# Odd mixer of a two-layer decoder trunk: when a block's result is split into its parts

## The chip, the cores and the metric

The kernel runs on one core of a Trainium2 chip (trn2). The metric is the device time of one launch in microseconds. All of it is one program with five engines: TensorE (PE; its weight loads are listed as PEld), VectorE (DVE), ScalarE (ACT), GpSimd (POOL) and SyncE (SP, which issues transfers). Each engine works through its own queue in order; semaphores tie the queues together.

## The reference

Two layers act on 256 positions of width 1024. Layer 0 has an attention and retention mixer, layer 1 the odd mixer, which the change touches. Each mixer is followed by a retrieval mixer ("peer").

```python
def short_conv_mixer(xn, w_in, conv_w, w_out):       # the odd mixer, layer 1; CONV_WIDTH is 3
    d = xn.shape[-1]
    bg, cg, hx = jnp.split(xn @ w_in, 3, axis=-1)
    u = cg * hx
    y = lax.conv_general_dilated(u, conv_w[:, None, :], window_strides=(1,),
                                 padding=[(CONV_WIDTH - 1, 0)],
                                 dimension_numbers=('NWC', 'WIO', 'NWC'),
                                 feature_group_count=d)
    return (bg * y) @ w_out

for layer in range(2):
    xn = rmsnorm(h, norm_mix[layer])
    h = h + (short_conv_mixer if layer % 2 else attn_retention_mixer)(xn, ...)
    h = h + peer(rmsnorm(h, norm_ffn[layer]), ...)
return rmsnorm(h, final_norm)
```

## The kernel before

The order on every engine is the order in which the program writes its instructions; no scheduler moves them.

**Weights.** All large matrices come through one stream of 128x1024 float32 tiles (class `Stream`). `_load` issues a tile's transfer from SP into one of eight `raw` buffers as soon as an earlier tile has given its buffer back. `_split` makes two parts of a tile: ScalarE casts it to a `hi` tile (line 146), and a subtraction of raw and `hi` gives a bfloat16 `lo` tile (line 148). The subtraction is on VectorE or, for tiles with a flag, on GpSimd. `next` hands a tile to a product and first calls `ahead`, which splits further tiles, up to four beyond the one that is asked for in this mixer.

**The products.** `u_tile` multiplies one weight tile with the 256 positions: 16 matmuls with `hi` (line 258), then 8 with `lo` (line 264). The result goes to a PSUM tile `hid`, of which there are two in turn; a product that needs one waits until VectorE has read the product before last in that ring.

**The odd mixer.** `odd_mixer` walks over 8 blocks of 128 channels. Block k takes three products, from the tiles 3k, 3k+1 and 3k+2 of its 24 input tiles. Tiles and products are given the same numbers here, so block 1 has the products 3, 4 and 5, and block 2 the products 6, 7 and 8. From tile 2 on the even tiles have their subtraction on VectorE and the odd ones on GpSimd.

- From product 3k VectorE makes `cg` (line 904).
- From product 3k+1 and `cg` it makes `u` (line 906), and from `u` the convolution `y` (lines 911 to 913).
- From product 3k+2 and `y` it makes `z` in PSUM (lines 918 and 919).
- `split_act` takes `z` apart: ScalarE casts it (`c2o`, line 653), VectorE subtracts that from `z` (line 656), and GpSimd makes a bfloat16 copy (`cbo`, line 658).

Block 0 is special: its first two products are run together by `u_pair` behind the end of the mixer before, its third follows, and three calls of `st.parts` split tiles 4, 5 and 6 between its steps. The third product of block 1 goes to another PSUM tile (`acc1`) instead of `hid`.

After the 8 blocks `v_phase` multiplies the parts of `z` with the 8 output tiles (lines 290 to 292), block by block, and the peer mixer of layer 1 follows.

Of the kernel before, what the change touches and what calls it, by code (L numbers as in the profile page):

```python
# [20 lines left out]
S = 256  # L21
D = 1024
ND = D // P
# [168 lines left out]
def trunk_kernel(ctx, tc, x, small, cst, mcst, ew_in, ew_out, ow_in, ow_out, wq, keys, pu, pv, pun, gains, out):  # L192
# [43 lines left out]
    def hid_tile(name):  # L236
        return ps_hid.tile([P, 512], F32, tag="hid", name=name)

    def side_tile(name):
        return ps_side.tile([P, 512], F32, tag="side", name=name)  # L240

    def acc_tile(n, name):
        return ps_acc.tile([P, 512], F32, tag=f"acc{n}", name=name)
# [3 lines left out]
    def nm(s):  # L247
        uid[0] += 1
        return f"{s}{uid[0]}"

    def u_tile(A2, Ab, ps=None, ahead=True):

        hi, lo = st.next(ahead)
        if ps is None:
            ps = hid_tile(nm("hid"))

        def one(k, s_):
            pe.matmul(ps[:, :S], hi[:, k * P:(k + 1) * P], A2[:, k, s_, :], start=k == 0 and s_ == 0, stop=False)  # L258

        for k in range(ND):  # L260
            one(k, 0)
            one(k, 1)
        for k in range(ND):
            pe.matmul(ps[:, :S], lo[:, k * P:(k + 1) * P], Ab[:, k, :], start=False, stop=k == ND - 1)  # L264
        return ps

    def u_pair(A2, Ab, tail, pss=None):


        ws = [st.next(ahead=False) for _ in range(2)]  # L270
        pss = pss or [hid_tile(nm("hid")) for _ in range(2)]
        for k in range(ND):
            for s_ in range(2):
                for (hi, lo), ps in zip(ws, pss):
                    pe.matmul(ps[:, :S], hi[:, k * P:(k + 1) * P], A2[:, k, s_, :], start=k == 0 and s_ == 0,
                              stop=False)
            tail(k)
        for (hi, lo), ps in zip(ws, pss):
            for k in range(ND):
                pe.matmul(ps[:, :S], lo[:, k * P:(k + 1) * P], Ab[:, k, :], start=False, stop=k == ND - 1)  # L280
        return pss
# [13 lines left out]
    def v_phase(n, part, each, norm):  # L295


        accs = [acc_tile(i, nm("acc")) for i in range(4)]
        for i in range(n - 2):
            each(i)  # L300
            w = st.next()
            p = part(i)
            for a in range(4):
                run(v_mm(w, p, accs[a], a // 2, a % 2, i == 0, False))
        each(n - 2)
        each(n - 1)
        ws = [st.next(), st.next(ahead=False)]
        st.ahead(0)
        ps = [part(n - 2), part(n - 1)]
        for a in range(4):  # L310
            for j in range(2):
                run(v_mm(ws[j], ps[j], accs[a], a // 2, a % 2, False, j == 1))
                if a == 3 and j == 0:
                    norm.amid()
            v.tensor_tensor(h[:, a // 2, (a % 2) * 512:(a % 2 + 1) * 512], accs[a],
                            h[:, a // 2, (a % 2) * 512:(a % 2 + 1) * 512], OP.add)
            norm.done(a, accs[a])
# [333 lines left out]
    def split_act(c2, cb, k, src, t, alone=False):  # L651

        act.copy(c2[:, k, 0, t], src)
        if alone:
            act.copy(cb[:, k, t], src)
        v.tensor_tensor(c2[:, k, 1, t], src, c2[:, k, 0, t].bitcast(F32), OP.subtract)
        if not alone:
            gp.tensor_copy(cb[:, k, t], c2[:, k, 0, t].bitcast(F32))
# [7 lines left out]
    def load_keys(l):  # L666
        KO = new_ko()
        for c in (slice(0, 4 * NK), slice(4 * NK, NPAIR * NK)):
            gp.dma_start(KO[:, c], keys[l][:, c])
# [211 lines left out]
    def odd_mixer(before, norm):  # L881
        with tc.tile_pool(name=nm("mix"), bufs=1) as mp, tc.tile_pool(name=nm("mix2"), bufs=2) as mp2:
            c2 = mp.tile([P, ND, 2, S], F32R, tag="c2", name="c2o")
            cb = mp.tile([P, ND, S], BF16, tag="cb", name="cbo")
            st.deep(mp2, 4 * ND, (1, 2))
            rs = mp.tile([P, 2, S], F32, tag="rs", name="rs")
            us = []
            for k in range(ND):
                w = [G[:, k * 3 + j:k * 3 + j + 1] for j in range(3)]
                if k == 0:  # L890
                    ps, pt = u_pair(xv["x2"], Xb, before.tail, [acc_tile(i, nm("hid")) for i in range(2)])
                    third = u_tile(xv["x2"], Xb, side_tile(nm("hid")), ahead=False)
                    rb = before.spread()
                    act.copy(rs[:, 0], rb)
                    v.tensor_tensor(rs[:, 1], rb, rs[:, 0], OP.mult)
                    load_keys(1)
                    us = [acc_tile(2 + i, nm("u"))[:, :S + 2] for i in range(2)]
                    for u in us:
                        v.memset(u[:, 0:2], 0.0)
                else:  # L900
                    ps = u_tile(xv["x2"], Xb)
                u = us[k % 2]
                cg = mp2.tile([P, S], F32, tag="cg", name=nm("cg"))
                v.tensor_tensor(cg, ps[:, :S], rs[:, 1], OP.mult)  # L904
                ps = u_tile(xv["x2"], Xb) if k else pt
                v.tensor_tensor(u[:, 2:], ps[:, :S], cg, OP.mult)
                if k == 0:
                    st.parts()
                    st.parts()
                y = mp2.tile([P, S], F32, tag="y", name=nm("y"))  # L910
                v.tensor_scalar(y, u[:, 0:S], w[0], None, op0=OP.mult)
                v.scalar_tensor_tensor(y, u[:, 1:S + 1], w[1], y, op0=OP.mult, op1=OP.add)
                v.scalar_tensor_tensor(y, u[:, 2:S + 2], w[2], y, op0=OP.mult, op1=OP.add)
                if k == 0:
                    st.parts()
                ps = u_tile(xv["x2"], Xb, acc_tile(1, nm("hid")) if k == 1 else None) if k else third
                z = (side_tile(nm("z")) if k else acc_tile(0, nm("z")))[:, :S]
                v.tensor_tensor(z, ps[:, :S], y, OP.mult)
                v.tensor_tensor(z, z, rs[:, 0], OP.mult)
                split_act(c2, cb, k, z, slice(0, S))  # L920

            def each(i):
                if i == 2:
                    norm.warm()

            v_phase(ND, lambda c: (c2[:, c, 0, :], c2[:, c, 1, :], cb[:, c, :]), each, norm)
# [575 lines left out]
    with tc.manual_schedule():  # L1502
        norms = [Norm(0)]
        nc.sync.dma_start(G, small)
        nc.sync.dma_start(C[:, :P], cst[:, :P])
        for th in range(2):
            (nc.scalar if th else nc.sync).dma_start(h[:, th, :], x[th])
        nc.sync.dma_start(C[:, P:], cst[:, P:])
        v.memset(Z, 0.0)
        act.activation(norms[0].w[:, 0, 6:7], Z[:, 0:1], AF.Sqrt)  # L1510
        for _ in range(3):
            st._load()
        busy(24)
        norms[0].first(hid_tile(nm("junk")))
        a = Norm(1)
        even_mixer(norms[0], a)
        b = Folded(2)
        peer(0, a, b)
        a = Norm(3)
        odd_mixer(b, a)  # L1520
        peer(1, a, Final(XF.rearrange("p k t -> p (k t)")[:, :D]))
# [38 lines left out]
```

## Time and profile before

| | |
|---|---|
| time, median of 3 runs (lowest to highest) | 1500.23 us (1499.57 to 1501.29) |
| time of the profiled execution | 1499.09 us |
| its span, first to last instruction | 1497.3 us |
| mean granted TensorE clock | 0.994 |
| busy share of the span: PE, DVE, ACT, POOL | 96%, 84%, 51%, 48% |
| blocks 1 to 7 of the odd mixer | about 775 to 838 us in the span |

Durations are from the one profiled execution. An entry in square brackets behind a row is the idle time of that engine before the row and what ended it.

### The profile page before, as it was taken

The page shows a single profiled execution, that of the slowest core. Times are in us where ns is not written, and L with a number is a line of the kernel's source. Part 1 is how long each engine was busy: PE and PEld are TensorE (multiplying, and loading weights), DVE is VectorE, ACT ScalarE, POOL GpSimd, SP SyncE. Part 2 cuts the span into 40 slices and gives each one's busy share as a digit, 9 for nine tenths or more (in the row PEclk, how much of TensorE's full clock was granted, in tenths as well). Part 3 has the DMA queues.
Part 4 walks back from the last instruction along what each step waited for, and adds up shares of the span by engine and source line. Part 5 has one row for each costly group of instructions (what it writes and reads, how often), then busy time and mean ns, then how long its engine had stood idle before and what let it go on. Part 6 is the DMA issues. An engine that isn't in the chain of part 4 may idle for free.

```text
span 1497.3 us, 30077 instructions
## 1 busy us (share of the span) xinstructions
PE 1437.4 (96%) x11158; PEld 1335.9 (89%) x11172; DVE 1251.5 (84%) x2469; ACT 761.5 (51%) x1825; POOL 725.1 (48%) x514
## 2 busy tenths in 40 slices
PE   9999999999999999999989999999999999999896
PEld 5667999999999998888888799999999999988885
DVE  5637999879998888888867589996999968888888
ACT  6556512257885545444563363212888835444454
POOL 6754545546665343444235364454566633434342
PEclk9999999999999999999999999999999999999999
DMA  8545899999999999999946578999999999999995
GB/s 321 196 153 201 301 391 408 397 409 403 408 405 408 403 399 409 409 401 408 394 174 209 185 250 320 408 408 397 407 407 399 409 398 402 401 408 406 397 405 225
DMA packets 147570, 532.99 MB, mean 356 GB/s; under 512 B 16992, under 2 KB 17248, under 8 KB 147424
## 3 DMA queue, kind: packets, MB, share of 16 engines
q1 hardware_dynamic: 72144, 258.36, 45.3%
q0 software_dynamic: 56704, 205.07, 34.8%
q10 hardware_dynamic: 18576, 67.64, 11.4%
q8 instruction: 88, 1.44, 0.4%
q14 instruction: 58, 0.48, 0.1%
HBM read 528.34 MB, written 1.05 MB: 354 GB/s over the span
## 4 chain that ended last, share of the span: by engine, by line
PE 39%; DMA 18%; DVE 17%; issue 16%; POOL 8%; ACT 3%; SPq 0%; POOLq 0%; ACTq 0%; DVEq 0%
PE hid L1356 17%; DMA raw<-pv 7%; POOL rows L964 5%; DMA rows<-pun,ig 4%; PE hid L258 3%; DMA grow<-pun,ig 2%; DVE rows L974 2%; POOL grow L964 2%; PE vo L1486 2%; DMA rows<-pv,ig 2%; PE ea L290 2%; PE ea L291 2%; PE ea L292 1%; PE hid L264 1%; PE vo L1482 1%
## 5 line engine op out<-in xcount | busy, mean ns | idle before, releaser
L1356 PE MATMUL hid<-xf,raw 128*128 128x160 f32 x3392 | 486.5, 301 | 6.4 <-DMA raw<-pu 4.0
L1356 PEld LDWEIGHTS hid<-xf,raw 128*128 128x128 f32 x3392 | 467.0, 191 | 9.0 <-issue 5.6
L1367 ACT CAST vhi<-raw 128x1024 fp32r<-128x1024 f32 x190 | 198.6, 1046 | 265.3 <-DMA raw<-pv 208.5
L1374 DVE TENSOR_TENSOR vlo<-raw,vhi 128x1024 bf16<-128x1024 f32 x190 | 231.9, 1223 | 81.3 <-ACT vhi L1367 58.8
L1486 PE MATMUL vo<-ko,vhi 128*128 128x320 f32 x1520 | 270.6, 320 | 26.8 <-DVE ko L1448 26.5
L964 POOL DMA_INDIRECT rows<-pv,ig x128 | 184.2, 1439 | 217.2 <-DVE gacc L989 179.8
L1486 PEld LDWEIGHTS vo<-ko,vhi 128*128 128x128 f32 x1520 | 224.4, 188 | 35.9 <-DVE ko L1448 35.4
L964 POOL DMA_INDIRECT rows<-pun,ig x128 | 169.4, 1324 | 135.7 <-DVE rows L974 65.6
L148 POOL TENSOR_TENSOR lo<-raw,hi 128x1024 bf16<-128x1024 f32 x70 | 168.5, 2417 | 83.2 <-ACT hi L146 80.1
L974 DVE SCALAR_TENSOR_TENSOR rows<-rows,xg 128x1024 f32<-128x1024 f32 x128 | 155.1, 1217 | 21.2 <-DMA rows<-pun,ig 17.9
L1389 ACT ACTIVATE hg<-hid 128x160 f32<-128x160 f32 (+14 forms) x240 | 62.5, 265 | 214.2 <-PE hid L1356 183.7
L989 DVE SCALAR_TENSOR_TENSOR gacc<-rows,ghid,gacc 128x1024 f32<-128x1024 f32 x124 | 158.6, 1279 | 1.1 <-DMA rows<-pv,ig 0.3
L1482 PE MATMUL vo<-hg,raw 128*128 128x160 f32 x1056 | 157.7, 302 | 0.8 <-DVE hg L1392 0.8
L964 POOL DMA_INDIRECT grow<-pv,ig x64 | 91.7, 1433 | 125.4 <-DVE gacc L989 115.6
L1482 PEld LDWEIGHTS vo<-hg,raw 128*128 128x128 f32 x1056 | 146.2, 191 | 1.2 <-DVE hg L1392 1.0
L1488 PE MATMUL vo<-hb,vlo 128*128 128x160 bf16 x1520 | 138.1, 234 | 0.0
L964 POOL DMA_INDIRECT grow<-pun,ig x64 | 81.2, 1268 | 78.1 <-DVE grow L974 45.0
L1488 PEld LDWEIGHTS <-vlo 128*128 128x128 bf16 x1520 | 100.5, 98 | 19.6 <-DVE vlo L1374 0.5
L1306 ACT ACTIVATE ko<-ko,idxT 128x128 f16<-128x128 f16 x320 | 101.7, 391 | 30.4 <-DVE ko L1292 30.3
L146 ACT CAST hi<-raw 128x1024 fp32r<-128x1024 f32 x100 | 102.3, 1047 | 17.4 <-issue 10.1
L258 PE MATMUL hid<-x,hi 128*128 128x256 f32 x800 | 107.4, 287 | 3.5 <-DVE cg L904 2.5
L258 PEld LDWEIGHTS hid<-x,hi 128*128 128x128 f32 x800 | 98.5, 190 | 4.5 <-ACT hi L146 2.7
(247 smaller groups left out, 2091.2 us busy)
## 6 DMA issues: line engine op xcount, KB each, us to landing
raw<-pu SPq DMA_DIRECT2D x212, 512.0 KB
raw<-pv SPq DMA_DIRECT2D x128, 512.0 KB
raw<-pv ACTq DMA_DIRECT2D x128, 512.0 KB
raw<-wq SPq DMA_DIRECT2D x32, 512.0 KB
raw<-ew_in SPq DMA_DIRECT2D x28, 512.0 KB
raw<-ow_in SPq DMA_DIRECT2D x24, 512.0 KB
hg<-pu SPq DMA_DIRECT2D x22, 512.0 KB
raw<-ew_out SPq DMA_DIRECT2D x8, 512.0 KB
```

The costliest lines, as they stand in the source:

```text
L146: self.nc.scalar.copy(hi, t)
L148: eng.tensor_tensor(lo, t, hi.bitcast(F32), OP.subtract)
L258: pe.matmul(ps[:, :S], hi[:, k * P:(k + 1) * P], A2[:, k, s_, :], start=k == 0 and s_ == 0, stop=False)
L964: gp.indirect_dma_start(self.row(s_), None, table, bass.IndirectOffsetOnAxis(IG[:, 0, s_ % STEPS:s_ % STEPS + 1].bitcast(U32), 0))
L974: v.scalar_tensor_tensor(r, r, 1.0, XG[:, q % 2, :], op0=OP.mult, op1=OP.mult, accum_out=w)
L989: v.scalar_tensor_tensor(self.acc[q], r, w, self.acc[q], op0=OP.mult, op1=OP.add)
L1356: pe.matmul(ps[:, :TD], w[k], XF[:, k, :], start=k == 0, stop=k == ND - 1)
L1367: act.copy(whi[j], raw)
L1374: v.tensor_tensor(wlo[j], raw, whi[j].bitcast(F32), OP.subtract)
L1482: pe.matmul(vo[b][:, :TD], w[:, b * P:(b + 1) * P], HG[:, i, :], stop=False, **m)
L1486: pe.matmul(vo[b][:, :2 * TD], hi[:, b * P:(b + 1) * P], hs, stop=i == NK - 1, **m)
L1488: pe.matmul(vo[b][:, :TD], lo[:, b * P:(b + 1) * P], hb, stop=i == NK - 1, **m)
```

## The change

The call of `split_act` for block k moves from the end of block k to block k+1, between that block's `cg` and its second product. The call for the last block stays behind the loop. No instruction is added or removed.

```diff
                 cg = mp2.tile([P, S], F32, tag="cg", name=nm("cg"))
                 v.tensor_tensor(cg, ps[:, :S], rs[:, 1], OP.mult)
+                if k:
+                    split_act(c2, cb, k - 1, z, slice(0, S))
                 ps = u_tile(xv["x2"], Xb) if k else pt
                 v.tensor_tensor(u[:, 2:], ps[:, :S], cg, OP.mult)
...
                 v.tensor_tensor(z, ps[:, :S], y, OP.mult)
                 v.tensor_tensor(z, z, rs[:, 0], OP.mult)
-                split_act(c2, cb, k, z, slice(0, S))
+            split_act(c2, cb, ND - 1, z, slice(0, S))
```

## Prediction

> **What bounds the kernel now.** I read the page first, then the windows around the odd mixer, then who waits for whom there, then each engine's timeline, row by row.
>
> ```profile
> span 1497.3 us, 30077 instructions
> ```
> ```profile
> 775.00:793.00 18.00, 14.47 (x120) 13.14 (x119) 14.70 (x25) 9.50 (x12) 11.68 (x9) 1.00 0.75 264
> 793.00:838.00 45.00, 45.00 (x386) 42.81 (x385) 31.22 (x52) 16.58 (x20) 22.98 (x14) 1.00 0.61 199
> 860.00:880.00 20.00, 19.74 (x161) 18.14 (x161) 16.62 (x65) 15.24 (x33) 12.92 (x10) 1.00 0.50 172
> 960.00:1000.00 40.00, 40.00 (x290) 40.00 (x290) 39.73 (x148) 8.35 (x21) 21.50 (x17) 0.98 1.03 409
> 1000.00:1100.00 100.00, 100.00 (x791) 99.50 (x791) 84.22 (x190) 54.28 (x192) 52.37 (x44) 1.00 1.03 403
> ```
>
> The columns are the stretch, its length, the busy time of PE, PEld, DVE, ACT and POOL, the granted clock, the DMA share and GB/s. From 793 to 838 us PE is busy for 45.00 of 45.00 us: nothing that moves on another engine can shorten that, and ScalarE's waits there cost nothing. Only from 775 to 793 us, in blocks 1 and 2, does PE stand still. So the waits view of 775 to 842 us has to be read with that in mind:
>
> ```profile
> ACT c2o L653 <- DVE z L919: 30.4, 8, 4.6
> PE hid L258 <- DVE cg L904: 2.5, 1, 2.5
> PE hid L258 <- DVE u L906: 1.0, 1, 1.0
> ```
>
> ScalarE's 30.4 us look like the prize, but PE's own waits are two, and they set the scale. PE's timeline (start, duration; each row is the `hi` half of a product) gives products 5, 6, 7, 8, 9 and, last, 12:
>
> ```profile
> 780.17 2.15 PE L258 MATMUL hid<-x,hi 128*128 128x256 f32 x16
> ...
> 783.24 2.15 PE L258 MATMUL hid<-x,hi 128*128 128x256 f32 x16
> ...
> 787.30 2.15 PE L258 MATMUL hid<-x,hi 128*128 128x256 f32 x16 [1.03 <-DVE u L906]
> ...
> 792.81 2.15 PE L258 MATMUL hid<-x,hi 128*128 128x256 f32 x16 [2.47 <-DVE cg L904]
> ```
> ```profile
> 795.60 2.15 PE L258 MATMUL hid<-x,hi 128*128 128x256 f32 x16
> ...
> 803.98 2.15 PE L258 MATMUL hid<-x,hi 128*128 128x256 f32 x16
> ```
>
> Undisturbed, a product starts 795.60 - 792.81 = 2.79 us behind the one before. Measured by that, product 6 is late by 0.28 us, product 7 by 1.27 and product 8 by 2.72: 4.27 us in all, the most that this change can win in the mixer. Product 7 takes the PSUM buffer that `u` of block 1 reads, product 8 the one that `cg` of block 2 reads. So the end is set by how early VectorE reaches these two.
>
> **What holds VectorE there.** Its rows are, in order: subtraction for tile 6, last step of z(0), cg(1), subtraction for tile 8, u(1), last step of z(1), subtraction for tile 10, cg(2).
>
> ```profile
> 779.09 2.00 DVE L148 TENSOR_TENSOR lo<-raw,hi 128x1024 bf16<-128x1024 f32 x1
> ...
> 781.46 0.43 DVE L919 TENSOR_TENSOR z<-z,rs 128x256 f32<-128x256 f32 x1
> ...
> 782.68 0.41 DVE L904 TENSOR_TENSOR cg<-hid,rs 128x256 f32<-128x256 f32 x1
> 784.23 2.58 DVE L148 TENSOR_TENSOR lo<-raw,hi 128x1024 bf16<-128x1024 f32 x1 [1.14 <-ACT hi L146]
> 786.73 0.42 DVE L906 TENSOR_TENSOR u<-hid,cg 128x256 f32<-128x256 f32 x1
> ...
> 789.29 0.43 DVE L919 TENSOR_TENSOR z<-z,rs 128x256 f32<-128x256 f32 x1
> ...
> 791.10 1.23 DVE L148 TENSOR_TENSOR lo<-raw,hi 128x1024 bf16<-128x1024 f32 x1 [0.52 <-ACT hi L146]
> 792.25 0.42 DVE L904 TENSOR_TENSOR cg<-hid,rs 128x256 f32<-128x256 f32 x1
> ```
>
> On ScalarE: casts of tiles 4, 5, 6; c2o(0); casts of 7, 8, 9; c2o(1); casts of 10, 11, 12.
>
> ```profile
> 775.13 2.95 ACT L146 CAST hi<-raw 128x1024 fp32r<-128x1024 f32 x3
> 781.93 0.37 ACT L653 CAST c2o<-z 128x256 fp32r<-128x256 f32 x1 [3.85 <-DVE z L919]
> 782.20 2.94 ACT L146 CAST hi<-raw 128x1024 fp32r<-128x1024 f32 x3
> 789.75 0.37 ACT L653 CAST c2o<-z 128x256 fp32r<-128x256 f32 x1 [4.61 <-DVE z L919]
> 790.02 2.94 ACT L146 CAST hi<-raw 128x1024 fp32r<-128x1024 f32 x3
> ```
>
> On GpSimd: subtraction for tile 5; cbo(0); subtractions for 7 and 9.
>
> ```profile
> 777.21 2.80 POOL L148 TENSOR_TENSOR lo<-raw,hi 128x1024 bf16<-128x1024 f32 x1 [0.77 <-ACT hi L146]
> 782.36 0.40 POOL L658 CAST cbo<-c2o 128x256 bf16<-128x256 f32 x1 [2.36 <-ACT c2o L653]
> 783.33 5.74 POOL L148 TENSOR_TENSOR lo<-raw,hi 128x1024 bf16<-128x1024 f32 x2 [0.56 <-ACT hi L146]
> ```
> ```profile
> 798.21 2.40 POOL L148 TENSOR_TENSOR lo<-raw,hi 128x1024 bf16<-128x1024 f32 x1 [0.56 <-ACT hi L146]
> ```
>
> The last row, tile 13, shows one such subtraction by itself, 2.40 us.
>
> So the casts of tiles 7 to 9 sit behind c2o(0), which waits for z(0); VectorE's subtraction for tile 8 waits for the second of them; it then takes 2.58 us where the one for tile 10 takes 1.23; and the subtraction for tile 10 again waits for a cast behind c2o(1). The 2.58 us are an exclusion: 1.22 us of VectorE's work between two subtractions of GpSimd gives 5.74 - 1.22 = 4.52 us for the two, 2.26 each, and 783.33 + 2.26 + 1.22 = 786.81 = 784.23 + 2.58. The two engines do not do these subtractions at once, and VectorE, waiting, got its turn before GpSimd's next one. Tile 6 shows the same: GpSimd ends at 780.01, VectorE 1.08 us later. [...]
>
> **The change part by part.** The same instructions are issued, and SP's and PE's orders stay as they are. ScalarE: per block one cast, of tile 3k+4, goes ahead of c2o(k-1), so the order becomes 4, 5, 6, 7; c2o(0); 8, 9, 10; c2o(1); 11. VectorE: `cg` of block k goes ahead of the subtraction for `c2o` of block k-1, and where tile 3k+4 is even, its `lo` does too. GpSimd: where tile 3k+4 is odd, its `lo` goes ahead of cbo(k-1). The transfers that wait for freed raw buffers only come earlier.
>
> *Cast of tile 7.* ScalarE is free at 775.13 + 2.95 = 778.08. The tile must be there:
>
> ```profile
> 758.65 1.28 SPq L131 DMA_DIRECT2D raw<-ow_in  x3
> 769.12 0.33 SPq L131 DMA_DIRECT2D raw<-ow_in  x1
> ```
> ```profile
> GB/s 342 80 15 0 259 360 375 284 120 7 0 0 0 178 288 0 0 0 11 269 353 308 422 406 306 397 317 29 226 324 284 240 251 73 320 160 248 255 273 149
> ```
>
> The second row has 40 slices of 1.125 us from 755 us on. Slices 5 to 9 carry 1398 x 1.125 = 1573 KB, the three tiles 7, 8 and 9, in by 765.1; slices 14 and 15 carry tile 10, in by 771.9. The cast runs from 778.08 to about 779.1.
>
> *Tile 7 on GpSimd.* It is ready at 779.1, but GpSimd is busy until 780.01 and VectorE waits since 779.09. With VectorE served first, as for tile 8 today, tile 6 still ends at 781.09 and z(0) at 781.89; tile 7 follows, 781.09 + 2.36 = 783.45 (2.36 lies between the 2.26 and the 2.40 from above).
>
> *Block 1.* cg(1) follows z(0) at once, about 781.92, so product 6 starts at its undisturbed 782.96. c2o(0) stays at 781.93, the cast of tile 8 takes the place of tile 7's at 782.20 and ends at 783.2. VectorE's subtraction for tile 8 finds GpSimd done at 783.45 and takes about 1.1, as for tile 6: it ends at 784.57, and u(1) starts at about 784.5 instead of 786.73. That is 0.98 us from the cast and 1.3 from the exclusion. Product 7 starts undisturbed at 785.75, behind u(1)'s end at 784.9.
>
> *Block 2.* u(1) to the end of z(1) takes 789.72 - 786.73 = 2.99 us of dependent steps: z(1) ends at 787.5. Tile 10's cast now runs right behind 8 and 9 and ends at 785.2 (its buffer is tile 5's, which product 5 reads until 782.32). So the subtraction for tile 10 starts at 787.5 instead of 791.10, if GpSimd's for tile 9 (from 784.57 + 0.40 for cbo(0), to about 787.4) is over. cg(2) starts 1.15 later, at 788.65 instead of 792.25: 3.6 us earlier, and product 8 with it, at 789.2.
>
> *What can shave it.* [...] No row shows who wins between a short cast and a waiting VectorE. The bounds are 2.9 and 3.6; I take half of the 0.40 off the upper: 3.4. This leaves PE 0.87 us of its 4.27.
>
> *What is moved and hidden.* The subtraction for c2o(k-1) now stands ahead of `u`, 0.42 us, and it waits for c2o, which stands behind a cast that waits for a `hi` buffer. That buffer is freed by product 3k-1, which z(k-1) needs as well, so the cast is over first. The cover in the later blocks:
>
> ```profile
> 799.12 2.58 DVE L148 TENSOR_TENSOR lo<-raw,hi 128x1024 bf16<-128x1024 f32 x1
> 801.62 0.42 DVE L906 TENSOR_TENSOR u<-hid,cg 128x256 f32<-128x256 f32 x1
> ```
>
> Here, in block 3, a collision of tile 14 with tile 13 on GpSimd already costs 1.36 us (2.58 - 1.22) and u(3) ends at 802.04, 1.94 us before product 12 needs its buffer at 803.98. So 0.42 us, or one collision in a block, is free; two in one block would stop PE by 2 x 1.36 - 1.94 = 0.78. c2o of the last block keeps its place, and `v_phase` needs the parts of block 6 long after.
>
> **Sum.** From product 9 on everything depends on PE's queue, the output products and the peer mixer included, so it moves as a whole. The profiled execution of 1499.09 us (span 1497.3, 1.8 around it) becomes 1495.7; that run lies 1.1 under the median of 1500.23, so the median becomes 1496.8. A difference of 0.2%, 3.0 us, is about what a measurement of this kernel can tell from no change; the forecast lies just beyond it.
>
> **The rivals.** [...] Chance 0.13.
>
> *The gain is lost in the transfers.* From 960 us the DMA share is 1.03 at 409 GB/s, and a stage bound by transfers ends when they do. For it: that stage is most of the rest. Against it: at 860 to 880 us the share is 0.50, so the bound stage does not begin by itself, but when buffers come free,
>
> ```profile
> SPq L131 <- POOL lo L148: 43.1, 15, 5.9
> ```
>
> and these come earlier with the rest (the row is SP's waits from 755 to 860 us). If it holds all the same, 1500.2. Chance 0.12.
>
> *Slower: second collisions.* [...] Chance 0.05.
>
> **How the numbers follow.** The forecast has 0.70. Its own range is 2.9 to 3.6 us, widened by the runs' spread (0.66 below the median, 1.06 above). The low end is the full 4.27 of PE's stalls, 1496.0, less 0.3 of spread: 1495.7. The high end takes in the first rival: 1499.2; the other two, 0.17, are left out. Faster by over 3.0 us: about three quarters of 0.70 and a little of luck elsewhere, 0.54. Within 0.2%: the rest of it, the first two rivals and half of the third, 0.42. Slower by over 0.2%: 0.04.
>
> **What would show it.** In the changed profile product 6 follows 5 by 2.79 us, 7 follows 6 by 2.79, and 8 follows 7 by 3.2 to 4.2; VectorE's subtraction for tile 8 takes about 1.2 us; a cast stands between 778 and 779.1 us; PE is full from product 9 to the end of the mixer. [...] The prediction is wrong if the gaps go and the time stays, or if new gaps stand behind product 9.

## The result, and the profile after

The changed kernel took 1495.57 us (median of 11 runs, 1494.1 to 1497.11) against 1499.89 us for the kernel before in the same comparison (11 runs, 1497.86 to 1503.21): ratio 0.9972, 95% interval 0.9964 to 0.998, so 4.3 us less. Forecast were 1496.8 us and a range from 1495.7: the direction and the size were right, the time lies 0.13 us under the range's low end.

The windows of the mixer in the changed kernel (busy time of PE, PEld, DVE, ACT, POOL; granted clock; DMA share; GB/s):

```profile
775.00:793.00 18.00, 17.51 (x151) 16.53 (x151) 15.00 (x29) 10.62 (x15) 15.86 (x9) 1.00 0.77 278
793.00:838.00 45.00, 45.00 (x379) 42.12 (x377) 27.64 (x51) 18.57 (x22) 22.98 (x15) 1.00 0.58 199
```

PE is busy for 17.51 of the first 18 us, where it was 14.47. The waits from 775 to 842 us:

```profile
ACT c2o L653 <- DVE z L921: 13.3, 8, 3.8
...
PE hid L258 <- DVE cg L904: 0.5, 1, 0.5
DVE c2o L656 <- ACT c2o L653: 0.4, 1, 0.4
```

ScalarE's wait for z fell by 17 us, far more than the kernel won. VectorE's waits for c2o, 0.44 us in each block, all but went; in the kernel before their row was

```profile
DVE c2o L656 <- ACT c2o L653: 3.5, 8, 0.4
```

The 3.1 us by which they fell lie close to what the kernel won, so they are a rival for its cause; an experiment below takes them away alone. PE's own two waits are now one of 0.5 us. PE's timeline, products 5 to 8:

```profile
781.77 2.15 PE L258 MATMUL hid<-x,hi 128*128 128x256 f32 x16
...
784.56 2.15 PE L258 MATMUL hid<-x,hi 128*128 128x256 f32 x16
...
787.35 2.15 PE L258 MATMUL hid<-x,hi 128*128 128x256 f32 x16
...
790.88 2.14 PE L258 MATMUL hid<-x,hi 128*128 128x256 f32 x16 [0.49 <-DVE cg L904]
```

Products 6 and 7 follow after 2.79 us each, undisturbed; product 8 after 3.53, so 0.74 us late. The delays went from 4.27 to 0.74 us: 3.53 won. Product 5 itself starts 1.60 us later than in the profile before. All of that lies ahead of what the change touches: product 2 already starts at 772.94 instead of 771.34. So the spans differ by 2.0 us only, and a comparison of the two spans would have hidden nearly half of the gain.

VectorE (subtraction for tile 8, u(1), last step of z(1), subtraction for tile 10, cg(2)), then ScalarE, then GpSimd:

```profile
784.88 1.48 DVE L148 TENSOR_TENSOR lo<-raw,hi 128x1024 bf16<-128x1024 f32 x1 [0.52 <-ACT hi L146]
786.29 0.42 DVE L908 TENSOR_TENSOR u<-hid,cg 128x256 f32<-128x256 f32 x1
...
788.84 0.43 DVE L921 TENSOR_TENSOR z<-z,rs 128x256 f32<-128x256 f32 x1
789.18 1.22 DVE L148 TENSOR_TENSOR lo<-raw,hi 128x1024 bf16<-128x1024 f32 x1
790.31 0.42 DVE L904 TENSOR_TENSOR cg<-hid,rs 128x256 f32<-128x256 f32 x1
```
```profile
776.73 3.90 ACT L146 CAST hi<-raw 128x1024 fp32r<-128x1024 f32 x4
783.53 0.37 ACT L653 CAST c2o<-z 128x256 fp32r<-128x256 f32 x1 [2.91 <-DVE z L921]
783.80 2.95 ACT L146 CAST hi<-raw 128x1024 fp32r<-128x1024 f32 x3
```
```profile
778.81 6.13 POOL L148 TENSOR_TENSOR lo<-raw,hi 128x1024 bf16<-128x1024 f32 x2 [0.22 <-ACT hi L146]
784.89 0.39 POOL L658 CAST cbo<-c2o 128x256 bf16<-128x256 f32 x1
```

Four casts now stand in front of the first c2o instead of three. Tile 8's subtraction starts right behind its cast and takes 1.48 us instead of 2.58; tile 10's starts behind z(1) without waiting for anything. GpSimd's tiles 5 and 7 take 6.13 us, two subtractions with VectorE's tile 6 between them: without its 1.22 us they leave 2.45 us each, and tile 6 ends at 782.69, 2.25 us ahead of GpSimd's 784.94. So the waiting VectorE was served first, as for tile 8 in the kernel before.

### The profile page after: what moved, and what is told of

Same layout as the page of the kernel before. It is cut to its first block, busy times and chain, and to the rows that moved or that the text cites. A ratio compares the mean times of both kernels' runs of the same rounds, so it can differ in the third digit from the quotient of the medians.

```text
span 1495.3 us, 30076 instructions
## 1 busy us (share of the span) xinstructions
PE 1436.5 (96%) x11158; PEld 1334.2 (89%) x11172; DVE 1247.0 (83%) x2469; ACT 760.6 (51%) x1825; POOL 730.8 (49%) x514
## 4 chain that ended last, share of the span: by engine, by line
PE 38%; DMA 18%; DVE 17%; issue 16%; POOL 8%; ACT 2%; another core or an unknown queue 0%; SPq 0%; POOLq 0%; DVEq 0%; ACTq 0%
PE hid L1358 17%; DMA raw<-pv 8%; POOL rows L966 5%; PE hid L258 4%; DMA rows<-pun,ig 3%; DMA grow<-pun,ig 3%; DVE rows L976 3%; POOL grow L966 2%; DMA rows<-pv,ig 2%; PE vo L1488 2%; DMA raw<-pu 2%; PE ea L290 2%; PE hid L264 2%; PE ea L291 2%; PE ea L292 1%
## 5 line engine op out<-in xcount | busy, mean ns | idle before, releaser
L966 POOL DMA_INDIRECT rows<-pv,ig x128 | 188.6, 1474 | 214.6 <-DVE gacc L991 174.0
L1308 ACT ACTIVATE ko<-ko,idxT 128x128 f16<-128x128 f16 x320 | 101.8, 390 | 52.6 <-DVE ko L1294 52.4
L1311 ACT ACTIVATE ko<-ko,idxT 128x128 f16<-128x128 f16 x320 | 101.1, 387 | 0.0
```

The source lines that it names most:

```text
L966: gp.indirect_dma_start(self.row(s_), None, table, bass.IndirectOffsetOnAxis(IG[:, 0, s_ % STEPS:s_ % STEPS + 1].bitcast(U32), 0))
```

## The experiments

All are compared with the kernel before, on one chip per group. "Mixer" is the time from the start of product 5 to the first output product (line 290) in the run's profile, read from PE's timeline; "delays" are the times by which products 6, 7 and 8 follow later than 2.79 us. The ratio with its interval is the one on record; it is not exactly the quotient of the two medians.

| run | delays, us | mixer, us | median, us (kernel before) | ratio, 95% interval |
|---|---|---|---|---|
| kernel before | 0.28, 1.27, 2.72 | 57.33 | | |
| changed, first comparison | 0, 0, 0.74 | 53.79 | 1495.57 (1499.89) | 0.9972 (0.9964 to 0.998) |
| again | 0, 0, 0.73 | 53.80 | 1496.50 (1501.32) | 0.9970 (0.996 to 0.998) |
| again2 | 0, 0, 0.72 | 53.78 | 1497.37 (1500.92) | 0.9978 (0.9969 to 0.9988) |
| rest_only | 0, 1.54, 2.72 | 57.32 | 1500.59 (1501.32) | 0.9997 (0.9986 to 1.0008) |
| cast_only | 0.27, 0, 0.78 | 54.13 | 1496.56 (1501.32) | 0.9965 (0.9952 to 0.9978) |
| cg_first | 0, 0, 0 | 54.79 | 1496.44 (1501.32) | 0.9967 (0.9956 to 0.9979) |
| cg_first_b2 | 0, 0, 0 | 53.07 | 1496.58 (1500.76) | 0.9972 (0.9962 to 0.9983) |
| null | 0.27, 1.28, 2.72 | 57.32 | 1499.89 (1500.76) | 1.0001 (0.999 to 1.0012) |
| pad | 0, 0, 0.73 | 107.56 | 1550.88 (1500.76) | 1.0329 (1.0316 to 1.0343) |
| pad2 | 0, 0, 0.72 | 57.64 | 1500.93 (1500.92) | 1.0005 (0.9994 to 1.0015) |
| idle | 0, 0, 0.73 | 69.24 | 1516.60 (1500.92) | 1.0103 (1.0083 to 1.0122) |

**Which part does it.** The call was taken apart. `rest_only` leaves ScalarE's cast where it was and moves the two other instructions:

```diff
+                if k:
+                    split_act(c2, cb, k - 1, z, slice(0, S), cast=False)
                 ps = u_tile(xv["x2"], Xb) if k else pt
...
-                split_act(c2, cb, k, z, slice(0, S))
+                split_act(c2, cb, k, z, slice(0, S), rest=False)
+            split_act(c2, cb, ND - 1, z, slice(0, S), cast=False)
```

> One part alone: ScalarE's cast of z stays where it was, only VectorE's subtraction and GpSimd's copy move one product later. Theory A says the gain comes from ScalarE's next weight cast getting ahead of the cast of z: product 6 loses its 0.28 us of delay, but u of block 1 still waits for tile 8, whose cast still comes third behind c2o, so products 7 and 8 start as before: 0 to 0.3 us under the kernel before. The rival (VectorE's wait of 0.44 us for c2o in front of cg is what counts, 8 x 0.44 = 3.5 us in sum) says about 3.5 us.

`cast_only` leaves all three at the end of the block, but has the next weight tile split ahead of them:

```diff
+                if k < ND - 1:
+                    st.ahead(1)
                 split_act(c2, cb, k, z, slice(0, S))
```

> The other part alone: the parts of z stay at the end of their block, but the split of the next weight tile (its cast, and its subtraction) is written ahead of them. Theory A: tile 8's and tile 10's casts come one place earlier as in the changed kernel; cg of block 2 still stands behind VectorE's subtraction for c2o of block 1 (0.42 us), so product 8 is 0.3 to 0.5 us later than in the changed kernel: 3.0 us under the kernel before. The rival (VectorE's waits) says about 0.

The waits of `rest_only` from 775 to 843 us:

```profile
ACT c2o L654 <- DVE z L924: 30.5, 8, 4.6
...
DVE lo L148 <- ACT hi L146: 8.7, 6, 1.7
...
PE hid L258 <- DVE cg L907: 2.5, 1, 2.5
...
PE hid L258 <- DVE u L911: 1.3, 1, 1.3
...
DVE c2o L659 <- ACT c2o L654: 0.4, 1, 0.4
```

In the kernel before the second of these rows was

```profile
DVE lo L148 <- ACT hi L146: 5.1, 7, 1.7
```

VectorE's wait for c2o has all but gone (3.5 to 0.4 us, one wait in place of eight), its wait for the `hi` casts has grown (5.1 to 8.7 us), and PE still waits for `cg` and for `u`. `rest_only` won nothing: product 6 wins its 0.28 us, product 7 loses it again, the mixer stays at 57.32 us, the ratio is 0.9997. `cast_only` shortens the mixer by 3.20 us of the changed kernel's 3.54, and its time cannot be told from the changed kernel's; its product 8 comes only 0.04 us later than there, where 0.3 to 0.5 us were expected. `rest_only` and the changed kernel differ in ScalarE's order alone. So the gain comes from one ScalarE cast per block getting ahead of the cast of z, and moving the parts of z is one way to get that. VectorE's waits of 0.44 us for c2o, 3.5 us in sum and thus as long as the gain, are worth nothing: what they free, VectorE spends waiting for the cast behind.

**What is left.** `cg_first` also moves the split of tile 3k+4 behind `cg`; `cg_first_b2` does so in block 2 alone:

```diff
-                    ps = u_tile(xv["x2"], Xb)
+                    ps = u_tile(xv["x2"], Xb, ahead=False)
...
                 if k:
+                    st.ahead(0)
                     split_act(c2, cb, k - 1, z, slice(0, S))
```

> The changed kernel, with the split of tile 3k+4 written behind cg of block k instead of ahead of its product, still ahead of the parts of z. In the changed kernel product 8 is the only one that still waits (0.74 us), for cg of block 2, which stands behind the subtraction for tile 10. Theory A: cg of block 2 comes about 1.1 us earlier, product 8 starts undisturbed, and all of the 4.27 us are gone: 0.7 us under the changed kernel, 4.3 under the kernel before, with u of block 2 still ahead of product 9. If the subtraction of tile 10 is only late somewhere else, the delay shows up before product 9 or 10 and the time equals the changed kernel's.

> The changed kernel with the later split in block 2 alone, so that the collisions of the later blocks stay as they are in the changed kernel. Theory A: product 8 starts 2.79 us behind product 7 (3.53 in the changed kernel), no gap of PE comes after it, and the mixer is 0.74 us shorter than in the changed kernel, 4.27 us shorter than before; time 0.7 us under the changed kernel, which is about 0.05% and hard to see in the times. If the collision comes back whatever the block, there is a gap of 1 to 2 us before a product between 9 and 18.

Product 8 loses its last delay in both, but in `cg_first` product 16 then follows product 15 after 4.51 us, 1.72 too late. Its PE, VectorE and GpSimd rows show why:

```profile
812.91 2.15 PE L258 MATMUL hid<-x,hi 128*128 128x256 f32 x16 [1.47 <-DVE z L921]
```
```profile
803.44 3.40 DVE L148 TENSOR_TENSOR lo<-raw,hi 128x1024 bf16<-128x1024 f32 x1
...
808.99 3.43 DVE L148 TENSOR_TENSOR lo<-raw,hi 128x1024 bf16<-128x1024 f32 x1
```
```profile
803.38 2.38 POOL L148 TENSOR_TENSOR lo<-raw,hi 128x1024 bf16<-128x1024 f32 x1 [1.30 <-ACT hi L146]
808.96 2.38 POOL L148 TENSOR_TENSOR lo<-raw,hi 128x1024 bf16<-128x1024 f32 x1 [3.20 <-ACT hi L146]
```

Twice in one block GpSimd's subtraction starts 0.06 and 0.03 us ahead of VectorE's, which then ends 1.08 us behind the end of GpSimd's: 3.4 us instead of 1.22, 2.2 more each time, where the prediction had 1.36 us as the price of a collision. Two collisions in one block are what the prediction's paragraph on the cover priced at 0.78 us; here they cost 1.72. Two subtractions of GpSimd ahead of one of VectorE's do not show here. `cg_first_b2` has no such gap and the shortest mixer of all, 53.07 us. That is 4.26 us under the kernel before; by time, 0.9972, it cannot be told from the changed kernel.

**Does the mixer's time reach the end, and is there more?** The first comparison's 4.3 us against 3.5 us in the trace led to these three, and to the two repetitions of the changed kernel.

> The changed kernel once more, unaltered. Theory A (the mixer alone): PE's three delays before products 6, 7 and 8 shrink from 4.27 us to about 0.74 us, the rest of the program only moves, so the time is 3.5 us under the kernel before (about 0.24%), and the 4.3 us of the first comparison were scatter. Theory B (the later stages add to it): the time stays 4.3 us or more under it (0.29% or more).

> The kernel before against itself, unaltered. It shows how far apart two medians of one kernel lie in this measurement: ratio 1.000, and an interval of about 0.1% to either side if the two comparisons of the changed kernel (4.3 and 4.8 us) are 3.5 us and scatter. If it lies off 1.000 by 0.05% or more, the comparison itself leans to the second kernel. Inside the mixer products 6, 7 and 8 are late by 4.27 us again.

`pad` and `pad2` run the `hi` half of product 10 more often (the lines are from `pad`; `pad2` has `extra=2`):

```diff
-        for k in range(ND):
-            one(k, 0)
-            one(k, 1)
...
+        for n in range(1 + extra):
+            for k in range(ND):
+                one(k, 0, n < extra)
+                one(k, 1, n < extra)
...
-                ps = u_tile(xv["x2"], Xb) if k else pt
+                ps = u_tile(xv["x2"], Xb, extra=28 if k == 3 else 0) if k else pt
```

> The changed kernel, with the hi half of the second product of block 3 run 28 times over ahead of the pass that counts: 28 x 1.99 = 55.7 us more of PE's queue in the mixer, and nothing else. Theory A says what happens in the mixer reaches the end one to one: the time is 55.7 us over the changed kernel, about 52 over the kernel before. Theory B, that later stages give 4.3 to 4.8 us for 3.5 in the mixer (1.2 to 1.35 times), says 68 to 75 us over the changed kernel. If the transfers behind the mixer set the end by themselves, much less than 55.7.

> The changed kernel, with the hi half of the second product of block 3 run twice over ahead of the pass that counts: 2 x 1.99 = 3.98 us of PE's work, in place of the 3.53 us of gaps that the change took away. Theory A: 0.45 us over the kernel before, the same within the interval. If the change also won about 1 us outside PE's queue in the mixer, 0.5 to 1 us under the kernel before.

> The changed kernel unaltered, on the same chip as the two others, as their reference. Theory A: 3.5 us under the kernel before; with what the first two comparisons and the three relatives gave, 4.4 to 4.7.

The kernel before against itself gave 1.0001 with 0.11% to either side, 1.6 us: the scatter of these times is nearly half of what is to be measured. `pad` lengthened the mixer by 53.77 us in its trace (107.56 against 53.79 in the changed kernel; a repeat took 1.92 us, not the 1.99 expected) and the time by 50.1 over the kernel before. With the 3.5 us that were won that is 53.7, so all of it; measured against the medians of `again2`, `again` and the first comparison, which belong to other groups, it is 53.5, 54.4 and 55.3. Later stages do not multiply what the mixer wins, and the transfers do not swallow it. In `pad2` product 10's half runs three times (48 matmuls):

```profile
795.87 5.99 PE L258 MATMUL hid<-x,hi 128*128 128x256 f32 x48
```

This put 3.85 us of work back, and the time was that of the kernel before (1.0005). The three comparisons of the changed kernel gave 4.3, 4.8 and 3.6 us; 3.5 us is a ratio of 0.9976, inside all three intervals. The 4.8 us of `again` is what its theory B said; `pad` speaks against that theory.

**Does a gap cost more than it lasts?** `idle` brings gaps of PE back into blocks 3 to 7:

```diff
-                v.tensor_scalar(y, u[:, 0:S], w[0], None, op0=OP.mult)
+                for _ in range(11 if k > 2 else 1):
+                    v.tensor_scalar(y, u[:, 0:S], w[0], None, op0=OP.mult)
```

> The changed kernel; in blocks 3 to 7 VectorE writes the first term of y eleven times over instead of once (10 x 0.52 = 5.2 us a block), so that PE has to stand still in the middle of the mixer as it did before the change, only more often. With a cover of about 2 us a block PE's gaps should come to 2 to 4 us a block, S = 10 to 20 us in all, to be read from the trace. Theory A (idle time of PE costs what it lasts): the time is the changed kernel's plus S. Theory C (the change won 4.4 to 4.7 us with 3.5 us of gaps because a gap costs PE more than it lasts, by its clock or by what starts again behind it): the changed kernel's plus 1.25 to 1.35 S, 4 to 6 us more than A for S = 15.

From product 5 to the first product behind the output projection the trace is 18.1 us longer than that of `again2` (95.43 against 77.31), and the time 19.2: what the trace shows is what it costs. But not all of it is gap. PE's timeline shows the products behind the gaps, and the windows their clock (the last three columns are the granted clock, the DMA share and GB/s):

```profile
807.09 3.66 PE L258 MATMUL hid<-x,hi 128*128 128x256 f32 x16 [2.32 <-DVE z L921]
...
820.48 3.49 PE L258 MATMUL hid<-x,hi 128*128 128x256 f32 x16 [3.25 <-DVE z L921]
```
```profile
832.93 2.55 PE L258 MATMUL hid<-x,hi 128*128 128x256 f32 x16 [2.31 <-DVE z L921]
...
845.12 2.15 PE L258 MATMUL hid<-x,hi 128*128 128x256 f32 x16 [1.99 <-DVE z L921]
...
855.43 0.50 PE L290 MATMUL acc<-hi,c2o 128*128 128x512 f32 x1 [2.40 <-DVE y L916]
```
```profile
805.00:810.00 5.00, 2.91 (x14) 2.94 (x15) 3.99 (x8) 1.32 (x2) 2.07 (x2) 0.71 0.09 15
...
820.00:825.00 5.00, 4.52 (x26) 4.28 (x27) 2.73 (x5) 2.27 (x3) 0.40 (x1) 0.66 0.45 130
...
845.00:850.00 5.00, 4.88 (x41) 4.75 (x42) 3.92 (x8) 2.37 (x3) 3.29 (x2) 1.00 0.29 107
```

Behind a wait of 2.32 or 3.25 us the half product takes 3.5 to 3.7 us instead of 2.15, at a clock of 0.66 to 0.71; behind one of 1.99 us it takes 2.15, at 1.00. Behind the wait of 2.31 us two half products take 2.55 and 2.58 us, and the clock from 835 to 840 us is 0.72; behind one of 2.40 us, among the output products, it is 1.00 (from 850 to 875 us). In the mixer the four gaps delay PE by 10.9 us and the slow matmuls by 4.6 more; the fifth gap adds 2.7 in the output products. So 13.5 us of gaps cost 18.1 us in the trace, 1.34 times their length, as theory C said. The kernel before has a wait of 2.47 us in front of product 8, and its two profiles so far showed product 9 after 2.79 and 2.78 us behind it, the first at a clock of 1.00. Four more profiles asked whether it is always so, three of the kernel before and one of `rest_only`, whose gaps are nearly the same:

> The kernel before, unaltered, one more profile. Theory C (the gaps before products 7 and 8, 1.27 and 2.72 us, sometimes bring down the clock that PE is granted behind them, as gaps of 2.5 to 3.6 us did in the kernel with idle blocks): in some of these profiles the first product behind the gap takes 0.8 to 1.5 us longer (its hi half 3 to 3.7 us instead of 2.15) and the granted clock from 792 to 798 us is under 1. Theory A: 2.15 us and a clock of 1.00 every time, as in the profiles so far.

> The kernel before again, the same question as in the profile before this one: by theory C a slower product 7, 8 or 9 behind the gaps in some of the profiles, by 0.8 to 1.5 us; by theory A in none.

> The kernel before again, the same question: by theory C a slower product behind the gaps in some of the profiles; by theory A in none.

> The kernel in which only the subtraction and the copy of the parts move: its gaps before products 7 and 8 are 1.54 and 2.72 us. By theory C a slower product behind them in some of the profiles, by 0.8 to 1.5 us; by theory A in none.

In `look1` and `look3` products 6 to 9 are as before, and the mixer is 57.33 us. In `look2` it is 58.91, in `look4` 58.93. PE's timeline of `look2`, products 8 and 9 with their `lo` halves, and its windows:

```profile
795.03 2.53 PE L258 MATMUL hid<-x,hi 128*128 128x256 f32 x16 [2.47 <-DVE cg L904]
797.37 1.93 PE L264 MATMUL hid<-xb,lo 128*128 128x256 bf16 x8
798.95 2.60 PE L258 MATMUL hid<-x,hi 128*128 128x256 f32 x16
```
```profile
792.00:796.00 4.00, 1.53 (x14) 1.26 (x12) 2.93 (x6) 3.18 (x4) 2.08 (x2) 1.00 0.55 199
796.00:800.00 4.00, 4.00 (x23) 3.48 (x23) 2.71 (x5) 0.00 (x0) 0.80 (x1) 0.57 0.83 265
800.00:804.00 4.00, 4.00 (x36) 3.88 (x36) 2.18 (x4) 2.37 (x3) 2.73 (x2) 1.00 0.33 120
```

From 796 to 800 us PE is busy all the time and does 23 matmuls where the windows of the other profiles have 36 or 37: the granted clock is 0.57. Product 9 follows product 8 after 3.92 us instead of 2.79, product 10 after 3.25: 1.59 us lost. So these gaps cost more than they last in 2 of 7 profiles (one of five of the kernel before, one of two of `rest_only`). Behind product 8 nothing is lost in the seven profiles of the changed kernel (three), `cast_only`, `cg_first`, `cg_first_b2` and `pad2`: their longest delay there is 0.78 us, and product 9 follows after 2.78 to 2.80 us. The mean over the seven is 2 x 1.59 / 7 = 0.45 us; with the 3.53 us this makes an estimate of 4.0 us, a ratio of 0.9973, beside the 0.9972, 0.9970 and 0.9978 measured.

That the clock falls behind these gaps in some executions is shown. How often it does in the timed runs is not; seven profiles give the share only roughly. The granted clock of whole executions leans the same way: it is 0.992 in `look2` and `look4` and 0.993 to 0.995 in the other five profiles. Over the timed runs it averages 0.9933 for the kernel before (64 runs) and 0.9941 for the changed one (the 23 of `again` and `again2`), but 0.9938 in the 12 runs of `null`, so it gives no share either. The rest, about 0.2 us between 4.0 and the mean of the three comparisons, is within the scatter.

## Why the prediction was right or wrong

- **The bound.** That PE's queue sets the mixer's end, and that only the delays before products 6, 7 and 8 can be won, held: PE is full from product 9 on in the changed kernel, and `rest_only`, which took VectorE's waits in front of `cg` away and left 4.26 us of these delays, won nothing.
- **The sum.** 3.4 us forecast, 3.53 measured in the trace, with bounds of 2.9 and 3.6. Products 6 and 7 came undisturbed; product 8 after 3.53 us, forecast 3.2 to 4.2. Counted from product 5, u(1) starts 0.2 us and cg(2) 0.1 us later than worked out. The step that no row showed was a short cast on GpSimd against a waiting VectorE: cbo(0) started at 784.89, 0.01 us behind the subtraction for tile 8, which took 1.48 us instead of 1.1 to 1.2. The 0.40 us for cbo(0) in the forecast and the 0.3 us that its lower bound has beyond them are the author's estimates, and no run shows them as such: tile 8's subtraction took 0.26 us more than the 1.22 of tile 10's, and tile 10's started right behind z(1), with GpSimd's tile 9 over at 788.61 (785.88 and 2.73 us).
- **VectorE first between two subtractions of GpSimd.** Right, by the 6.13 us of tiles 5 and 7. The range's high end of 1499.2 takes in a first rival, the author's estimate for the case that GpSimd goes on with tile 7 while VectorE waits with tile 6; no run shows this term, and in the changed kernel tile 6 took 1.99 us.
- **The way to the end.** One to one, as forecast: from the first product behind the output projection to the end there are 636.28 us before and 636.22 after, and over the changed kernel `pad` passed on 53.7 of the 53.77 us that it added and `pad2` 3.6 of 3.85, both within the scatter. The second rival (1500.2) falls.
- **Second collisions.** Not in the changed kernel, but at once in `cg_first`, at a higher price than forecast (1.72 us against 0.78).
- **What failed: the low end.** The step was "4.27 us in all, the most that this change can win in the mixer", from which the range ended at 1495.7. It counted a gap at its length. In 2 of 7 profiles the gap was followed by slow matmuls that lost another 1.59 us, so these delays cost 5.9 us there, and the 3.53 us taken away were worth about 4.0 on the mean, by the estimate above. The prediction read the granted clock of 1.00 behind the gaps in one profile and did not ask whether it is so in every execution. The other half of the miss is the base: the sum went from the median of three runs, 1500.23 us, and the comparison's own median of the kernel before was 1499.89; the 0.3 us that the range kept for this is small beside the 1.6 us by which the kernel before can differ from itself. From the base 1499.89 the same sum ends at 1495.3 and takes in the measured 1495.57. The miss is 0.13 us, while the comparison only places the gain between 3.0 and 5.4 us, which holds the forecast 3.4 as well. So it stays open how much of the miss each of the two terms made, and on which side of the range's end the time fell is in part luck.

## What to carry to other kernels

Where one engine both prepares the next operands and finishes the last result, write the preparation first: here one cast of about 1 us per block that waited in the queue behind a result cost the matrix engine 3.5 us in all, while the waits of the finishing steps themselves cost nothing as long as nobody needs them. Read the gain from the delays of the engine that sets the end, product by product, and not from the spans or from the longest list of waits: here 30 us of waits on ScalarE were worth 3.5 us, and the spans of two single profiles showed 2.0. A gap in TensorE's work should be priced at its length and a share of the slow matmuls that may follow it, which one profile may not show: here they cost 1.59 us behind a wait of 2.47 us in 2 of 7 profiles, and the shortest wait that was followed by them lasted 2.31 us.

## What had not been expected of the hardware

- The same gap of 2.72 us before product 8 was followed by product 9 after 2.78 to 2.80 us in five profiles, and by a clock of 0.57 (`look2`) and 0.62 (`look4`) from 796 to 800 us in two; in the one profile of `idle`, waits of 2.31, 2.32 and 3.25 us were followed by a clock of 0.72, 0.71 and 0.66 in the 5 us windows behind them, waits of 1.99 and 2.40 us by 1.00 (845 to 850 and 850 to 875 us).
- Of two subtractions that start within 0.06 us of each other in `cg_first`, GpSimd's went first, in 2.38 us, and VectorE's ended 1.08 us behind it: 3.40 us for work that took 1.22 elsewhere.
